# One load of two DRAM rows into both partition halves, made into two loads of one row each

## The chip, the cores and the metric

The kernel runs on one core of one Trainium2 chip. The metric is the device time of the whole program in microseconds (us). Engines are named as the profile names them: PE (TensorE, matrix products), DVE (VectorE), ACT (ScalarE), POOL (GpSimd), and SP (SyncE), which here does nothing but issue DMAs. "DMA engines" are the sixteen units that move the bytes.

## The reference, cut to what matters

An encoder of two layers on 1024 positions of width 1024. Layer 0 is a gated long convolution (Hyena), layer 1 a bidirectional Mamba-2 scan (SSD) with 32 heads in 4 groups, done in 8 chunks of 128 positions in both directions. Each layer has an input projection, the mixer, an output projection and a layer norm. The change lies in layer 1, in the part of the scan that reads the carried state:

```
a_cs = jnp.cumsum(adt, axis=-1)
...
y_off = jnp.einsum('bctgn,bcghpn,bcght->bctghp', cc, prev_states, jnp.exp(a_cs))
return (y_diag + y_off).reshape(b, L, h, p)
```

For one group, one chunk and one direction, `exp(a_cs)` is an array of 8 heads by 128 positions. It multiplies the product of state and `cc`, which has 8 heads by 64 channels by 128 positions.

## The kernel before, in words

All products are fp32 (split into a high and a low part where accuracy asks for three passes). The program is one long stream: layer 0 (about the first 1075 us of the profile), its output layer, and then layer 1, in which the projections of layer 1 (`flow`, matmuls at L763), the scan (`ssd_back`, `ssd_forth`) and the first part of the output projection (`Out.steps`, matmuls at L1203) are interleaved so that PE always has projection matmuls between the small steps of the scan. `advance` sets how many projection steps stand between two steps of the scan. The framework's scheduler then fixes one order for each engine; each engine, SP too, works its list strictly in order. All DMAs of the scan are issued by SP, in one list, but for small ones of POOL.

In the scan heads lie in pairs: partition 64*o + p of a tile holds channel p of head 2*i + o, with i (0 to 3) and the 128 positions along the row. So the exponentials of the even heads (o = 0) must stand on each of the partitions 0 to 63, and those of the odd heads (o = 1) on each of 64 to 127.

- `ssd_dt` computes the exponentials once and writes them by `spread` (L970) to the DRAM array `ecd`, of shape [direction, group, chunk, o, i, position]. One (direction, group, chunk) is two rows, o = 0 and 1, of 512 numbers, 2 KB each.
- `ssd_decay` (L1027 to L1032) loads such a pair of rows into a tile `ec` of 128 x 512 (256 KB), each row copied to 64 partitions. It is called once for each chunk but one, in 4 groups and 2 directions: 56 loads. Two buffers are there for each direction.
- `ssd_offset` (L1034 to L1041) multiplies: four matmuls at L1038, then one DVE multiplication at L1040 that reads `ec`. It is the only reader.

Names in the other lines that the prediction touches: `bxd` is a DRAM array into which the projected x, B and C are written (L980, L993), from which `bx` is loaded (L1002) and used by DVE at L1008 (`xw`); `ybd` holds the backward direction's result (stored L1105, loaded L1124); `y` is stored at L1162 and read back by the output projection as `tr` (L1317); `wr` is a raw weight block of 512 KB (L219), split by ACT (L227, L233) and DVE (L228, L234). L679 and L681 are the convolution on DVE and the SiLU on ACT whose result PE transposes at L988. L1073 and L1099 are matmuls of the scan's inner part, L1143 to L1160 the norm of its result.

Of the kernel before, what the change touches and what calls it, by code (L numbers as in the profile page):

```python
# [192 lines left out]
class Build:  # L193
# [833 lines left out]
    def ssd_decay(self, p, t, g, c, d):  # L1027

        ec = self.values(self.pb if d else p, f"ec{d}", 2).rearrange("p (i n) -> p i n", i=4)
        src = t["ecd"][d, g, c].rearrange("o i n -> o (i n)").unsqueeze(1).broadcast_to([2, 64, 512])  # L1030
        self.nc.sync.dma_start(out=ec.rearrange("p i n -> p (i n)"), in_=src)
        return ec  # L1032

    def ssd_offset(self, pool, g, c, state, bc, ec):  # L1034
# [515 lines left out]
```

## Time and profile before

| | us |
|---|---|
| median of 3 runs | 2164.39 |
| lowest and highest | 2164.05, 2165.11 |
| the profiled execution's own time | 2173.37 |
| its span, first to last instruction | 2171.6 |
| PE busy in the span | 2089.6 (96%) |
| DVE, ACT, POOL busy | 1567.9, 1136.4, 324.8 |

The profiled execution is 0.4% longer than the median of the runs. PE is busy nearly always, so what sets the time shows in its 82 us of idle time and in the stretches in which it works at the lower of its two clocks. Durations in the prediction are those of the profiled execution.

### The profile page before, as it was taken

To read this page: it belongs to the slowest core of one execution; us is meant where nothing else is said; L and a number is where in the kernel's file an instruction comes from. 1 tells how busy PE (TensorE), PEld (TensorE's weight loads), DVE (VectorE), ACT (ScalarE), POOL (GpSimd) and SP (SyncE) were. 2 spreads that over 40 slices of the span, in tenths; PEclk is the share of its full clock that TensorE was granted. 3 is DMA by queue.
4 is the path that set the end of the run, shared out by engine and by line. 5 is a ranking of instruction groups with operands and counts; after the bars stand their busy time and mean duration, and the time that the engine had idled before them with its cause. 6 is when DMAs were issued, how large, how long until landed. Compare 5 with 4: busy or idle time off the path is not lost.

```text
span 2171.6 us, 28748 instructions
## 1 busy us (share of the span) xinstructions
PE 2089.6 (96%) x9930; PEld 1661.5 (77%) x9930; DVE 1567.9 (72%) x2268; ACT 1136.4 (52%) x1665; POOL 324.8 (15%) x385
## 2 busy tenths in 40 slices
PE   7999999999999999999999998999999999989897
PEld 5777777888888888888777776776777777767676
DVE  7999977676777777767766564664777777667575
ACT  4787866465656556556544343554455555432231
POOL 0000000000000000000000101244344344433120
PEclk9999999999999999999999999999999999989998
DMA  6277887665656556556776325343454555557652
GB/s 208 103 237 249 266 263 240 202 197 168 199 165 186 171 159 194 182 181 197 270 275 217 121 66 157 110 122 119 124 154 150 168 160 162 161 172 245 229 174 93
DMA packets 269631, 391.92 MB, mean 180 GB/s; under 512 B 31767, under 2 KB 168727, under 8 KB 268845
## 3 DMA queue, kind: packets, MB, share of 16 engines
q1 hardware_dynamic: 255741, 382.99, 55.8%
q0 software_dynamic: 13744, 7.09, 1.4%
q8 instruction: 79, 1.29, 0.2%
q14 instruction: 67, 0.55, 0.1%
HBM read 269.10 MB, written 120.85 MB: 180 GB/s over the span
## 4 chain that ended last, share of the span: by engine, by line
PE 74%; DMA 11%; DVE 8%; ACT 3%; issue 2%; SPq 1%; POOL 1%; POOLq 0%; DVEq 0%; ACTq 0%
PE pj L270 28%; PE pj L763 16%; PE pj L1203 8%; PE f L250 3%; PE f L252 3%; PE f L251 3%; DMA wr<-l_w_out 2%; PE f L1038 2%; PE pk L1203 2%; DMA tr<-y 2%; PE f L1015 1%; PE f L1099 1%; PE f L1073 1%; DMA bxd<-tr 1%; DVE wl L234 1%
## 5 line engine op out<-in xcount | busy, mean ns | idle before, releaser
L270 PE MATMUL pj<-xth,wh 128*128 128x512 f32 x1024 | 326.5, 398 | 1.8 <-ACT xth L233 1.8
L270 PE MATMUL pj<-xtl,wh 128*128 128x512 f32 x1024 | 326.5, 396 | 1.4 <-DVE xtl L234 1.4
L270 PE MATMUL pj<-xth,wl 128*128 128x512 f32 x1024 | 324.8, 394 | 0.0
L234 DVE TENSOR_TENSOR wl<-wr,wh 128x1024 fp32r<-128x1024 f32 x152 | 192.2, 1267 | 139.6 <-ACT wh L233 138.8
L233 ACT CAST wh<-wr 128x1024 fp32r<-128x1024 f32 x152 | 159.4, 1049 | 165.7 <-PE pj L1203 58.5
L270 PEld LDWEIGHTS pj<-xtl,wh 128*128 128x128 f32 x1024 | 192.7, 189 | 45.7 <-DVE xtl L234 2.4
L270 PEld LDWEIGHTS pj<-xth,wl 128*128 128x128 f32 x1024 | 193.0, 189 | 44.2 <-issue 0.5
L270 PEld LDWEIGHTS pj<-xth,wh 128*128 128x128 f32 x1024 | 189.4, 189 | 42.2 <-ACT xth L233 3.4
L763 PE MATMUL pj<-h1th,wh 128*128 128x512 f32 x640 | 212.8, 406 | 0.9 <-DVE cv L679 0.9
L763 PE MATMUL pj<-h1tl,wh 128*128 128x512 f32 x640 | 203.8, 395 | 0.0
L763 PE MATMUL pj<-h1th,wl 128*128 128x512 f32 x640 | 202.8, 394 | 0.0
L234 DVE TENSOR_TENSOR xl<-bs,xh 128x512 fp32r<-128x512 f32 x192 | 129.7, 687 | 51.9 <-ACT xh L233 51.1
L233 ACT CAST xh<-bs 128x512 fp32r<-128x512 f32 x192 | 117.8, 621 | 69.8 <-DMA bs<-vs 28.7
L763 PEld LDWEIGHTS pj<-h1th,wh 128*128 128x128 f32 x640 | 117.6, 189 | 38.6 <-issue 15.8
L567 DVE SCALAR_TENSOR_TENSOR cv<-pj,cw,cv 128x960 f32<-128x960 f32 x192 | 139.3, 745 | 4.9 <-ACT cv L564 2.8
L763 PEld LDWEIGHTS pj<-h1tl,wh 128*128 128x128 f32 x640 | 120.8, 189 | 26.9 <-issue 1.5
L763 PEld LDWEIGHTS pj<-h1th,wl 128*128 128x128 f32 x640 | 121.1, 190 | 25.7 <-issue 0.2
L1187 POOL TENSOR_SCALAR rs<-mv 128x1 f32<-128x1 f32 x16 | 6.3, 395 | 896.5 <-DMA yr<-y 707.9
L679 DVE SCALAR_TENSOR_TENSOR cv<-pj,cw,cv 128x1023 f32<-128x1023 f32 (+1 forms) x96 | 122.6, 1277 | 5.8 <-ACT cv L676 5.2
L1086 POOL TENSOR_TENSOR m<-m,dm 128x512 f32<-128x512 f32 x64 | 93.9, 1466 | 74.2 <-DVE m L1078 73.7
L1081 POOL TENSOR_TENSOR dm<-ident,dco 128x512 f32<-128x512 f32 x64 | 69.5, 1086 | 189.3 <-DVE dco L1066 137.2
L389 DVE TENSOR_TENSOR kr<-f,dec 64x512 f32<-64x512 f32 x128 | 87.9, 687 | 3.6 <-ACT dec L386 1.1
(292 smaller groups left out, 4195.4 us busy)
## 6 DMA issues: line engine op xcount, KB each, us to landing
wr<-w SPq DMA_DIRECT2D x104, 512.0 KB
k<-kd SPq DMA_DIRECT2D x256, 128.0 KB
wr<-l_w_out SPq DMA_DIRECT2D x64, 512.0 KB
ask<-asb SPq DMA_DIRECT2D x64, 256.0 KB
bs<-ask SPq DMA_DIRECT2D x64, 256.0 KB
kd<-asb SPq DMA_DIRECT2D x64, 256.0 KB
as<-asb SPq DMA_DIRECT2D x64, 256.0 KB
bs<-as SPq DMA_DIRECT2D x64, 256.0 KB
```

What stands on the lines that cost most here:

```text
L233: self.nc.scalar.copy(h, src)
L234: self.nc.vector.tensor_tensor(out=l, in0=src, in1=h.bitcast(F32), op=ALU.subtract)
L250: mm(out, ah, bh, start=start, stop=False)
L251: mm(out, ah, bl, start=False, stop=False)
L270: self.nc.tensor.matmul(ps[:, t], lhs[:, k], rhs[:, k, t], start=st, stop=sp)
L389: (nc.gpsimd if 2 * q + i in PM else nc.vector).tensor_tensor(out=ks[q ^ i][r], in0=ps[r], in1=dec[r], op=ALU.mult)
L567: nc.vector.scalar_tensor_tensor(out=acc[:, o], in0=ps[:, i], scalar=cw[:, w:w + 1], in1=acc[:, o], op0=ALU.mult, op1=ALU.add)
L679: nc.vector.scalar_tensor_tensor(out=acc[:, o], in0=ps[:, i], scalar=cw[:, w:w + 1], in1=acc[:, o], op0=ALU.mult, op1=ALU.add)
L763: nc.tensor.matmul(ps[:, c], lhs[:, k], rhs[k // 4][:, k % 4, c], start=st, stop=sp)
L1081: nc.gpsimd.tensor_tensor(out=dm, in0=self.ident.unsqueeze(1).broadcast_to([128, 4, 128]), in1=dco[:, h4:h4 + 4].unsqueeze(2).broadcast_to ...
L1086: nc.gpsimd.tensor_tensor(out=m, in0=m, in1=dm, op=ALU.add)
L1203: self.nc.tensor.matmul(po[hf], lhs[:, t], rhs[:, 512 * hf:512 * hf + 512], start=s, stop=e)
```

## The change: two loads in place of one

```
     def ssd_decay(self, p, t, g, c, d):
 
         ec = self.values(self.pb if d else p, f"ec{d}", 2).rearrange("p (i n) -> p i n", i=4)
-        src = t["ecd"][d, g, c].rearrange("o i n -> o (i n)").unsqueeze(1).broadcast_to([2, 64, 512])
-        self.nc.sync.dma_start(out=ec.rearrange("p i n -> p (i n)"), in_=src)
+        for o in range(2):
+            src = t["ecd"][d, g, c, o].rearrange("i n -> (i n)").unsqueeze(0).broadcast_to([64, 512])
+            self.nc.sync.dma_start(out=ec[64 * o:64 * o + 64].rearrange("p i n -> p (i n)"), in_=src)
         return ec
```

The source of the old load has three dimensions, 2 rows x 64 repeats x 512 numbers; that of each new load has two, 64 repeats x 512 numbers. The same bytes go to the same places. Lines below L1031 move down by one. The numbers of instructions on PE, DVE, ACT and POOL stay; SP issues 56 DMAs more.

SP's list at the start of the scan, before (names: `ec_...` is one buffer of the tile, `dwh` the exponentials in SBUF, the rest as above; a trailing x2 means two alike in a row):

```order
L970 DMA ecd<-dwh 8x4x128 x4
L1031 DMA ec_13935<-ecd 128x1x512
L1031 DMA ec_14115<-ecd 128x1x512
L219 DMA wr<-w 128x1024
L993 DMA bxd<-tr 128x4x128 x2
L1002 DMA bx<-bxd 128x896
```

SP's list at the same place with the change:

```order
L970 DMA ecd<-dwh 8x4x128 x7
L219 DMA wr<-w 128x1024
L1032 DMA ec_13942<-ecd 64x512 x2
L1032 DMA ec_14124<-ecd 64x512 x2
L993 DMA bxd<-tr 128x4x128 x2
L1002 DMA bx<-bxd 128x896
```

Each load has become two of 64 rows, and the weight load `wr` has moved ahead of them; the two stores of `tr` still stand behind them.

SP's list some 560 us later, in the output projection's stretch, before (`wr<-l_w_out` is a weight block of the output projection):

```order
L219 DMA wr<-l_w_out 128x1024
L1031 DMA ec_17283<-ecd 128x1x512
L1162 DMA y_68<-y 128x4x128
L1031 DMA ec_17289<-ecd 128x1x512
L219 DMA wr<-l_w_out 128x1024
L1124 DMA y<-ybd 128x512
```

And with the change:

```order
L219 DMA wr<-l_w_out 128x1024
L1032 DMA ec_17324<-ecd 64x512 x2
L1163 DMA y_68<-y 128x4x128
L1032 DMA ec_17331<-ecd 64x512 x2
L219 DMA wr<-l_w_out 128x1024
L1125 DMA y<-ybd 128x512
```

Here nothing has moved but that each load is two. In the last 200 us of the scan a few neighbours on DVE, ACT and SP change places, and one matmul on PE (L1015) moves ahead of seven of L1203.

## Rows read from the trace of the kernel before

**Rows 1.** The page: busy time, and the chain that ended last by engine.

```profile
PE 2089.6 (96%) x9930; PEld 1661.5 (77%) x9930; DVE 1567.9 (72%) x2268; ACT 1136.4 (52%) x1665; POOL 324.8 (15%) x385
...
PE 74%; DMA 11%; DVE 8%; ACT 3%; issue 2%; SPq 1%; POOL 1%; POOLq 0%; DVEq 0%; ACTq 0%
```

**Rows 2.** Waits of PE, 1316 to 2103 us: total us, times, longest.

```profile
PE f L988 <- ACT cv L681: 15.4, 3, 9.7
PE f L1073 <- DVE ss L1153: 9.4, 3, 4.3
PE f L1151 <- POOL dwh L1147: 7.1, 1, 7.1
PE f L1073 <- DVE y L1160: 6.1, 5, 2.4
```

**Rows 3.** Chain in order of time, its DMA legs: start, us from issue to landing.

```profile
1319.29 7.89 DMA bxd<-tr
...
1340.13 10.81 DMA bxd<-tr
1350.96 2.99 DMA bx<-bxd
...
1494.90 8.35 DMA ybd<-y
1503.26 2.64 DMA y<-ybd
...
1894.83 9.90 DMA wr<-l_w_out
...
2074.88 11.71 DMA tr<-y
```

**Rows 4.** SP's timeline at three of these legs: start, us, line, operation.

```profile
1335.35 1.10 SPq L1031 DMA_DIRECT2D ec<-ecd  x2
1336.51 2.97 SPq L219 DMA_DIRECT2D wr<-w  x1
1339.58 3.30 SPq L993 DMA_DIRECT2D bxd<-tr  x2
...
1492.87 0.51 SPq L1031 DMA_DIRECT2D ec<-ecd  x1
...
1893.46 0.51 SPq L1031 DMA_DIRECT2D ec<-ecd  x1
1894.83 0.35 SPq L219 DMA_DIRECT2D wr<-l_w_out  x1
```

**Rows 5.** Windows in which mainly such DMAs ran; the last two numbers: DMA share, GB/s.

```profile
64.25:65.25 1.00, 1.00 (x6) 0.76 (x5) 1.00 (x3) 1.00 (x3) 0.00 (x0) 1.00 0.57 178
211.50:212.30 0.80, 0.80 (x6) 0.63 (x5) 0.80 (x3) 0.80 (x1) 0.00 (x0) 1.00 0.87 330
...
1462.00:1464.00 2.00, 2.00 (x22) 1.48 (x20) 0.00 (x0) 0.00 (x0) 0.00 (x0) 1.00 0.13 47
```

**Rows 6.** Issues on SP by line: ns least/median/most.

```profile
L1031 SPq DMA_DIRECT2D ec<-ecd x56: 486/507/859, 1316.4 to 2074.3; - x56
...
L367 SPq DMA_DIRECT2D bs<-l_filt_w_out x16: 472/568/596, 15.5 to 214.7; - x16
```

**Rows 7.** Windows by stage: us, then busy PE, PEld, DVE, ACT, POOL; clock, DMA, GB/s.

```profile
1316.00:1530.00 214.00, 198.63 (x973) 153.31 (x971) 117.91 (x157) 101.27 (x128) 72.25 (x76) 0.95 0.40 120
1530.00:1820.00 290.00, 286.36 (x1496) 221.29 (x1495) 223.39 (x315) 148.58 (x194) 123.19 (x131) 0.99 0.51 154
1820.00:2103.00 283.00, 256.36 (x1272) 199.86 (x1272) 187.71 (x301) 100.84 (x148) 93.35 (x104) 0.96 0.62 194
1970.00:2045.00 75.00, 74.36 (x387) 59.19 (x387) 44.66 (x74) 17.84 (x31) 19.16 (x23) 1.00 0.71 228
```

**Rows 8.** The six windows at half clock from 1316 to 2103, three and their sum.

```profile
1351.40:1361.60 10.20, 3.03 (x11) 2.76 (x12) 3.85 (x4) 2.23 (x3) 0.00 (x0) 0.50 0.75 246
1515.40:1525.50 10.10, 9.17 (x24) 6.53 (x25) 3.59 (x7) 6.09 (x9) 1.81 (x2) 0.50 0.38 105
1566.50:1569.90 3.40, 3.40 (x10) 2.62 (x9) 3.40 (x6) 0.49 (x1) 0.00 (x0) 0.50 0.28 99
...
sum 44.00, PE 31.15 PEld 24.12 DVE 26.86 ACT 17.86 POOL 8.83; mean PE 5.19 PEld 4.02 DVE 4.48 ACT 2.98 POOL 1.47
```

**Rows 9.** The chain in the first output layer, which has no such loads.

```profile
1063.92 2.61 DMA yr<-y
...
1078.41 8.74 DMA wr<-l_w_out
1090.43 8.18 DMA yr<-y
```

**Rows 10.** SP's own waits, 1316 to 2103 us: total us, times, longest.

```profile
SPq L1031 <- DVE y L1040: 38.9, 24, 8.6
...
SPq L970 <- DMA ec<-ecd: 3.3, 1, 3.3
```

## The prediction

> **What bounds the kernel now.** I began with the page [rows 1]: PE is busy 96% of the span and holds 74% of the chain that ended last, but 11% of that chain is DMA. In a kernel bound by PE those DMA legs are the places where PE ran out of work. So next I asked who kept PE waiting in the stretch in which the changed loads are issued, 1316 to 2103 us. The windows by stage [rows 7] give its idle time: 214.0 - 198.6 = 15.4 us up to 1530, 290.0 - 286.4 = 3.6 us up to 1820, 283.0 - 256.4 = 26.6 us up to 2103, together 45.6 us. The table of PE's waits [rows 2] names ACT, DVE and POOL as releasers. None of them is the cause: the chain in order of time [rows 3] shows that behind them stand DMAs that took 8 to 12 us from issue to landing. The same kinds of DMA need 2.6 to 3.0 us elsewhere in that chain (the two `bx` and `y` legs in the same group).
>
> SP's timeline [rows 4] shows what these long legs share: each was issued just behind an `ec` load. The stores of `tr` at 1339.58 stand behind two of them, the store of `ybd` at 1494.90 two microseconds behind one, the weights at 1894.83 one microsecond behind one. And the windows [rows 5] show what an `ec` load does. At 1462 to 1464 one ran alone: the DMA share is 0.13 of sixteen engines, that is two engines, and they moved 47 GB/s. Its 256 KB (262144 bytes) at 47 GB/s take 5.6 us. So the two-row load runs on two engines, one for each row, it seems, and whatever is split over all engines behind it waits for these two. A DMA of 2.6 to 3.0 us becomes one of 8 to 9 us (8.35 in [rows 3]), and two `ec` loads in a row make it 11 (10.81).
>
> **The change, part by part.** *The shape.* Each load becomes two of 64 rows. The trace has a repeated source, the 128-row load of `delta`, which filled 64.25 to 65.25, and loads of 64 rows into tile halves from SP, which filled 211.5 to 212.3 [rows 5]. They ran at shares of 0.57 and 0.87, so on at least 9 and 14 engines, at 178 and 330 GB/s. At these rates the 256 KB of an `ec` pair take 1.5 or 0.8 us in place of 5.6. I take the worse, which shares the repeated source: every `ec` load keeps the engines 4 us less, and all sixteen alike, so that a DMA behind it is late by 1 to 1.5 us and not by 5 to 6.
>
> The Trainium skill speaks against this change. Its page "SBUF — State Buffer", section "Can I just issue two DMAs to hit both halves?", says that a DMA on half the partitions reaches half the ports and that two such DMAs serialize (it measured 6% more than one), and the rules of "DMA: Bandwidth & Descriptors" advise one transfer of 128 partitions. By that rule the gain would be nothing and the sum the time before. It compares with a full-width load, though, and the row at 1462 shows that the old load isn't one. The same page on DMA, section "Why a DMA increments its semaphore by 16 and not by 1", says that a DMA gets the largest number of engines up to 16 that divides the slowest dimension of both sides: 2 before, 16 after. The two engines at 1462 agree; that the new form gets 16, no run here shows yet.
>
> *The start of the scan, 1316 to 1530.* There 15.4 us of idle are the three waits for L681 [rows 2]: 11 us in two of them (behind the stores at 1319 and 1340), 4.4 in the third (behind `ybd` at 1494.90). After each PE fell to its lower clock of 1.2 GHz, shown as 0.50 [rows 8], in which it was busy 3.03 and 9.17 us; at 2.4 GHz that work takes half, so the clock costs another 6.1 us. With `tr` stored in about 3 us and not 8 and 11, the whole string from `tr` over `bx` to L1008 and L681 is done 7.89 + 10.81 - 2 x 3 = 12.7 us earlier, against 11 of idle; with `ybd` stored in 3 and not 8.35, DVE goes on 5 us earlier, against 4.4. Both stalls go, and nothing on PE is late next, since it has projection matmuls there. Term: 15.4 + 6.1 = **21.5 us**.
>
> *The middle, 1530 to 1820.* `ec` loads run here as everywhere, but PE is idle for 3.6 us alone; the waits are those for L1160 [rows 2], a burst of DVE work with no long DMA ahead of it. Also its window at half clock (3.40 us busy, 1.7 lost) stays. Term: **0**, at the most 3.6 + 1.7 = 5.3.
>
> *The end, 1820 to 2103.* Idle 26.6 us, and the other three windows at half clock hold 31.15 - 3.03 - 9.17 - 3.40 = 15.6 us of PE, which cost 7.8 [rows 8]. Of these 34.4 us some 2.5 are waits for L1160 that I leave, so 32 hang on long legs (`wr` of 9.90, `tr` of 11.71 [rows 3]). But here not all comes back. DVE is busy 188 of 283 us and the DMA share is 0.62 [rows 7]; with 25 us less for the same work both rise by a tenth, and the weight blocks of 512 KB delay each other without any `ec` load: in the first output layer legs of 8.74 and 8.18 us stand in the chain [rows 9]. On the other side, PE is busy 74.4 of 75 us in 1970 to 2045 at a DMA share of 0.71, the highest of the stages, so the share alone is no bound. Lower bound 0, upper bound 32; I take 70%, nearer the upper: **22 us**.
>
> *The added issues.* 56 more issues on SP, at the median of the 64-row loads 0.568 us [rows 6], make 32 us of SP's time in 787. SP waits far longer than that for others; its waits for L1040, which frees `ec`, alone come to 38.9 us [rows 10], and the second half doesn't wait again. A DMA behind a pair is issued 0.57 us later, which 4 us of earlier room cover; where the cover is thin I count **1 us** lost in all. Bounds: 0 and 32, if every issue lay on the path. The few neighbours that change places on DVE, ACT and SP I cost at nothing, for PE's list is the same but for one matmul; as bound either way I take the 6.1 us that the waits for L1160 [rows 2], which come from the order on DVE, cost in all.
>
> Sum: 21.5 + 22 - 1 = 42.5, rounded to 43. Against the profiled span, 2171.6 becomes 2129; the median of the runs is 9 us below the profiled execution, and the same 43 from 2164.4 give **2121 us**.
>
> **The rivals.** (a) *The end stays late.* The legs shrink, but the 512 KB weights, the `tr` loads and DVE keep PE waiting after 1820 as in [rows 9]. Then only the first term comes, with a little of the last: 21.5 to 26, or 2139 to 2143. For it: the busy DMA engines; against it: the stage at 0.71 with PE full.
>
> (b) *Everything comes back.* All 45.6 us of idle and 15.6 of clock, less a few: 55 to 60, so 2104 to 2109. For it: nearly every long leg in the chain is behind an `ec` load. Against it: DVE's own bursts.
>
> (c) *The halves serialize, or run on few engines too.* Then nothing lands sooner and the time is 2164, within 0.2%. Against it: 330 GB/s in [rows 5] for loads of the very shape. (This is what the page "SBUF — State Buffer" of the Trainium skill, as told above, would lead one to expect.)
>
> (d) *SP becomes the late one: slower.* SP works in order; 0.57 us more ahead of every DMA behind an `ec` load, and each extra DMA takes one of SP's completion semaphores, whose next user waits for its landing, as L970 did for an `ec` load, 3.3 us [rows 10]. A dozen legs of the chain, each later by 0.57, make 7 us, 2171; all 56 make 2196. It decides if the halves don't free the engines by at least 0.57 us sooner than the 5.6 of now, so only with (c).
>
> **How the numbers follow.** The forecast (gain 34 to 52, 2112 to 2130) gets 0.55, (a) 0.19, (b) 0.17, (c) 0.05, (d) 0.04. A measurement of this kernel can tell 0.2%, 4 us. Faster: 0.91; same: 0.05; slower: 0.04. The range reaches from (b)'s lower end, 2103, to (a)'s upper, 2143, and leaves out (c), (d) and the thin ends.
>
> **What would show it.** In the profile after: DMA share far over 0.13 while an `ec` pair runs alone; the legs `tr` at 1319 and 1340 and `ybd` at 1494 at 2.5 to 4 us; no idle of PE ahead of L988 before 1530, nor half clock; L970 not waiting for `ec`; PE idle from 1316 on down from 45.6 to about 15; L1160's waits still there. I am wrong if `ec` still occupies two engines, if `wr` and `tr` legs of 8 us and more remain in the last 200 us, or if PE's idle moves to waits for DVE.

## The result and the profile after

The changed kernel takes 2126.05 us (median of 4 runs, 2124.32 to 2128.08) against 2164.58 (2164.05 to 2165.11, 4 runs) before: a ratio of 0.9822, 95% interval 0.9805 to 0.9839, so 38.5 us faster. Timed again later beside other runs (the last experiment below) it took 2123.86 against 2169.34, ratio 0.9795 (0.9776 to 0.9814), 45.5 us faster. The profiled execution of the changed kernel took 2124.32 with a span of 2122.5.

The page of the changed kernel: busy time, and the chain that ended last by engine.

```profile
PE 2076.1 (98%) x9930; PEld 1654.5 (78%) x9930; DVE 1569.2 (74%) x2268; ACT 1136.8 (54%) x1665; POOL 326.6 (15%) x385
...
PE 84%; DVE 7%; DMA 3%; ACT 2%; issue 2%; POOL 1%; SPq 0%; POOLq 0%; DVEq 0%; ACTq 0%
```

Against [rows 1] PE's idle time in the span fell from 82 to 46 us, its busy time by 13.5 (the same 9930 matmuls, fewer of them at half clock), and the share of DMA in the chain from 11% to 3%. The other engines do the same work. Next the windows by stage. A stage is cut at the same matmuls of PE's list as in [rows 7], so that it holds the same work (the first count in brackets is PE's: 973, 1494 and 1273 here, 973, 1496 and 1272 there). The bounds 1316, 1530, 1820 and 2103 then lie at 1312.9, 1505.4, 1795 and 2054.

```profile
1312.90:1505.40 192.50, 192.50 (x973) 149.35 (x971) 117.57 (x157) 101.31 (x128) 71.90 (x76) 1.00 0.45 133
1505.40:1795.00 289.60, 286.49 (x1494) 221.29 (x1495) 222.25 (x315) 148.57 (x194) 124.98 (x132) 0.99 0.52 155
1795.00:2054.00 259.00, 250.73 (x1273) 196.97 (x1271) 190.54 (x301) 102.21 (x148) 94.47 (x104) 0.99 0.68 210
```

The first stage is 21.5 us shorter, the second 0.4, the third 24.0. Another 3.1 us were won before the first of the changed loads went out, and none after 2103: together 49.0 of the 49.1 us by which the span is shorter. Idle time of PE is length less busy time: 0 in the first stage (15.4 before), 3.1 in the second (3.6), 8.3 in the third (26.6). The rest is clock: in these stages the changed kernel has three half-clock windows and not six [rows 8], none of them in the first.

```profile
1542.10:1545.50 3.40, 3.40 (x10) 2.62 (x9) 3.40 (x7) 0.71 (x1) 0.00 (x0) 0.50 0.43 154
1876.60:1880.00 3.40, 3.04 (x11) 2.85 (x12) 3.40 (x7) 3.37 (x6) 1.02 (x2) 0.50 0.97 331
1927.80:1931.20 3.40, 3.40 (x10) 2.62 (x9) 1.89 (x3) 0.63 (x1) 2.03 (x3) 0.50 0.82 253
sum 10.20, PE 9.84 PEld 8.09 DVE 8.69 ACT 4.71 POOL 3.04; mean PE 3.28 PEld 2.70 DVE 2.90 ACT 1.57 POOL 1.01
```

The load itself: the first line is a stretch in which, but for a few small packets, the four halves of two `ec` tiles ran alone; then SP's timeline around two of the legs of [rows 3 and 4] (start, us, line, operation).

```profile
1330.30:1332.30 2.00, 2.00 (x12) 1.52 (x11) 0.39 (x1) 1.06 (x1) 0.00 (x0) 1.00 0.98 251
```

```profile
1327.76 2.42 SPq L1032 DMA_DIRECT2D ec<-ecd  x4
...
1333.20 0.92 SPq L993 DMA_DIRECT2D bxd<-tr  x2
...
1336.47 0.33 SPq L1002 DMA_DIRECT2D bx<-bxd  x1
...
1479.13 0.33 SPq L1106 DMA_DIRECT2D ybd<-y  x1
...
1482.35 1.27 SPq L1125 DMA_DIRECT2D y<-ybd  x3
```

The halves fill 0.98 of the sixteen engines where the old load filled 0.13 [rows 5], at 251 GB/s in place of 47. At this rate the 256 KB of a pair take 1.0 us in place of 5.6, between the 0.8 and 1.5 of the prediction. The two stores of `tr` still stand behind four halves, and the load of `bx` that needs them goes out 3.3 us after the first of them (11.4 before, 1339.58 to 1350.96 in [rows 4 and 3]); the load of `y` goes out 3.2 us after the store of `ybd` (8.35 before).

What is left shows in PE's waits (1312.9 to 2054: total us, times, longest) and in the chain's DMA legs after 1780 (start, us).

```profile
PE f L1074 <- DVE y L1161: 4.5, 4, 2.4
PE f L1152 <- POOL dwl L1148: 1.8, 2, 0.9
PE f L1160 <- ACT rs L1157: 1.7, 1, 1.7
PE f L1152 <- POOL dwh L1148: 1.2, 1, 1.2
```

```profile
1807.67 4.93 DMA bx<-bxd
...
1916.68 5.85 DMA bx<-bxd
...
1985.25 5.70 DMA y<-y
1992.01 2.81 DMA ec<-ecd
2001.13 5.79 DMA wr<-l_w_out
```

The 15.4 us for L988 of [rows 2] are gone, the waits for the norm's DVE work (L1160, now L1161) are not (6.1 us before, 4.5 now), and no DMA leg of this part of the chain is longer than 6 us.

### The profile page after: what moved, and what is told of

It reads as the page before. It is cut to its first block, busy times and chain, and to the rows that moved or that the text cites. A ratio compares the mean times of both kernels' runs of the same rounds, so it can differ in the third digit from the quotient of the medians.

```text
span 2122.5 us, 28822 instructions
## 1 busy us (share of the span) xinstructions
PE 2076.1 (98%) x9930; PEld 1654.5 (78%) x9930; DVE 1569.2 (74%) x2268; ACT 1136.8 (54%) x1665; POOL 326.6 (15%) x385
## 4 chain that ended last, share of the span: by engine, by line
PE 84%; DVE 7%; DMA 3%; ACT 2%; issue 2%; POOL 1%; SPq 0%; POOLq 0%; DVEq 0%; ACTq 0%
PE pj L270 32%; PE pj L763 19%; PE pj L1204 9%; PE f L250 3%; PE f L252 3%; PE f L251 3%; PE f L1039 2%; PE pk L1204 2%; PE f L1015 2%; PE f L1100 1%; PE f L1074 1%; DMA wr<-l_w_out 1%; DVE wl L234 1%; PE f L988 1%; PE f L383 1%
## 5 line engine op out<-in xcount | busy, mean ns | idle before, releaser
L270 PEld LDWEIGHTS pj<-xtl,wh 128*128 128x128 f32 x1024 | 192.7, 189 | 45.6 <-DVE xtl L234 2.1
L763 PE MATMUL pj<-h1th,wh 128*128 128x512 f32 x640 | 212.1, 405 | 0.9 <-DVE cv L679 0.9
L763 PE MATMUL pj<-h1tl,wh 128*128 128x512 f32 x640 | 202.6, 393 | 0.0
L763 PE MATMUL pj<-h1th,wl 128*128 128x512 f32 x640 | 202.0, 393 | 0.0
L763 PEld LDWEIGHTS pj<-h1th,wh 128*128 128x128 f32 x640 | 117.2, 188 | 38.2 <-issue 15.6
L763 PEld LDWEIGHTS pj<-h1tl,wh 128*128 128x128 f32 x640 | 120.0, 188 | 26.8 <-issue 1.5
L763 PEld LDWEIGHTS pj<-h1th,wl 128*128 128x128 f32 x640 | 120.1, 188 | 25.4 <-issue 0.2
```

The source lines that it names most:

```text
L270: self.nc.tensor.matmul(ps[:, t], lhs[:, k], rhs[:, k, t], start=st, stop=sp)
L763: nc.tensor.matmul(ps[:, c], lhs[:, k], rhs[k // 4][:, k % 4, c], start=st, stop=sp)
```

## The experiments

Theory A, the prediction's: what counts is on how many DMA engines a load of `ec` runs, because what stands behind a load on few engines waits for these. What the kernels vary for it is the slowest (outermost) dimension of the load's source, which is 2 before and 64 in each half of the change. Theory B: the cut itself helps, since two smaller DMAs, and the new order that the scheduler made of SP's, DVE's and ACT's lists, let other work in between. Six kernels keep the computation and write each exponential eight times to DRAM, with the same bytes loaded; then the number of engines and of loads can be chosen apart. Of each kernel the lines are shown that take the place of the old load; `m = 16 * d + 4 * g` is the first of the four rows of a direction and group. The store is the same in the six (one DMA of 32 x 8 x 128 in the place of 8 x 4 x 128):

```
-                nc.sync.dma_start(out=t["ecd"][:, :, c, o].rearrange("d g i n -> (d g) i n"),
-                                  in_=ec[r + o:r + 64:2, 128 * (c % 4):128 * (c % 4) + 128])
+                nc.sync.dma_start(out=t["ecd"][c, o].rearrange("k m n -> m k n"),
+                                  in_=ec[r + o:r + 64:2, 128 * (c % 4):128 * (c % 4) + 128].unsqueeze(1).broadcast_to([32, 8, 128]))
```

**One load on two engines** (as before, from copy 0; the lists of PE, DVE and ACT as before but for a handful of rows, SP's too but that the first `ec` loads and the `ecd` stores stand elsewhere):

```
+        src = t["ecd"][c, :, 0, m:m + 4].rearrange("o i n -> o (i n)").unsqueeze(1).broadcast_to([2, 64, 512])
```

> Control. The exponentials are written to DRAM in eight copies (16 stores of 128 KB in place of 16 KB), and one load of two rows x 64 repeats reads the first copy, as before. Theory A (the old load runs on two DMA engines, and all that is issued behind it waits for these two): the load is as narrow as before, so the time stays at 2164, plus 0 to 8 us for the larger stores at the start of the scan. Theory B (two issues instead of one, with the order that the scheduler then chooses, are what helps): also 2164 plus the stores. DMA share 0.13 while a load runs alone.

**Two loads on two engines** (64 rows each, from two copies; the lists of DVE and ACT as in the change but for a handful of rows):

```
+        for o in range(2):
+            src = t["ecd"][c, o, :2, m:m + 4].rearrange("k i n -> k (i n)").unsqueeze(1).broadcast_to([2, 32, 512])
+            self.nc.sync.dma_start(out=ec[64 * o:64 * o + 64].rearrange("p i n -> p (i n)"), in_=src)
```

> Two loads of 64 rows, as in the change, with the engine orders of the change, but each load's source is two copies x 32 repeats, so its slowest dimension is 2. Theory A: each half still runs on two engines; no gain, 2164 to 2175, slower than the control by up to 7 us for the added issues, DMA share 0.13 while a pair runs alone. Theory B: the whole gain, 2124 to 2135.

**One load on all engines** (sixteen rows, each repeated eight times; the lists of SP, DVE, ACT and POOL are those of the one load on two engines, row for row):

```
+        src = t["ecd"][c, :, :, m:m + 4].rearrange("o k i n -> (o k) (i n)").unsqueeze(1).broadcast_to([16, 8, 512])
```

> One load of 128 rows, in the engine orders of before, whose source is sixteen rows (two exponentials x eight copies) x 8 repeats. Theory A: it spreads over sixteen engines; the gain of the change without the split, 2120 to 2135 (up to 4 us better than the change for 56 issues fewer, up to 8 worse for the larger stores). Theory B: one issue and the old order, so 2164 and more.

**Two loads on all engines** (the change's own loads, from copy 0; those lists are again the ones of the two loads on two engines):

```
+        for o in range(2):
+            src = t["ecd"][c, o, 0, m:m + 4].rearrange("i n -> (i n)").unsqueeze(0).broadcast_to([64, 512])
+            self.nc.sync.dma_start(out=ec[64 * o:64 * o + 64].rearrange("p i n -> p (i n)"), in_=src)
```

> The fourth corner: two loads of 64 rows on sixteen engines, with the stores in eight copies. Theory A (engines used): within 8 us of the one wide load, 2120 to 2132, and over 30 below the two narrow loads. If the split by itself also cost the 9 us by which two narrow loads were slower than one narrow one, it is 2132; if that difference came from narrow loads queueing twice, it is 2123 to 2126.

| us, median (range; ratio to before with interval) | few engines | all engines |
|---|---|---|
| one load | 2154.72 (2153.76 to 2159.94; 0.9937, 0.9916 to 0.9958) | 2123.29 (2120.49 to 2124.61; 0.9791, 0.9773 to 0.9810) |
| two loads | 2164.11 (2158.92 to 2169.33; 0.9978, 0.9964 to 0.9991) | 2122.99 (2121.25 to 2124.21; 0.9782, 0.9761 to 0.9802) |

The two loads on all engines were timed beside runs of the kernel before at 2170.4 us, the other three beside runs at 2169.3.

Going from two engines to all gives 31.4 us with one load and 41.1 with two, with the same lists on each side. Cutting the load gives nothing with all engines (0.3 us) and loses 9.4 with few. So A is shown, and neither B's cut nor the change's lists of DVE and ACT are a gain of their own. Nor is it how many rows of DRAM a load reads: of the two loads the wide ones read one row each, the narrow ones two. Where the width counts can be seen in the first and the last stage, cut at the same matmuls, of one load on two engines and of one on all:

```profile
1317.40:1516.20 198.80, 194.18 (x975) 150.46 (x973) 118.48 (x156) 101.58 (x128) 71.52 (x75) 0.99 0.49 139
...
1807.30:2089.60 282.30, 259.25 (x1273) 202.26 (x1271) 186.30 (x301) 100.66 (x148) 94.01 (x104) 0.95 0.63 194
```

```profile
1316.70:1509.30 192.60, 192.60 (x975) 149.41 (x973) 117.09 (x156) 101.81 (x128) 71.36 (x75) 1.00 0.50 143
...
1797.10:2054.20 257.10, 249.69 (x1272) 195.87 (x1271) 188.64 (x301) 101.77 (x148) 97.21 (x104) 0.99 0.69 212
```

The last stage is 25.2 us shorter by width alone, the first only 6.2, for with one narrow load it is short already. That is the surprise in the first column, where no gain was expected: this kernel is 14.6 us below the runs of before beside it, and its first stage is 198.8 us long where the kernel before has 214.0. What fits this is SP's list:

```profile
1316.41 0.91 SPq L993 DMA_DIRECT2D bxd<-tr  x2
...
1328.08 0.59 SPq L1032 DMA_DIRECT2D ec<-ecd  x1
...
1346.22 0.34 SPq L1002 DMA_DIRECT2D bx<-bxd  x1
...
1356.86 0.53 SPq L1032 DMA_DIRECT2D ec<-ecd  x1
```

The first `ec` load goes out after the stores of `tr` at 1316 and not ahead of them, and the third, at 1356.86, behind the load of `bx`, where it stood ahead of the stores that this needs [rows 4]. So narrow loads that stand out of the way seem to do less harm; the larger stores differ too, and no run parts the two. Two narrow loads are 9.4 us worse than one mostly in the last stage (289.9 us against 282.3); whether the number of loads or the lists, which differ at once, make that isn't settled.

That the two loads were narrow shows in a stretch where one pair ran alone (two engines' share again):

```profile
1447.50:1449.50 2.00, 2.00 (x20) 1.53 (x20) 0.00 (x0) 0.00 (x0) 0.00 (x0) 1.00 0.13 49
```

**One load on four and on eight engines**, with the lists of one load on two, to see how the time goes with the width:

```
+        src = t["ecd"][c, :, ::4, m:m + 4].rearrange("o k i n -> (o k) (i n)").unsqueeze(1).broadcast_to([4, 32, 512])
```

> One load whose source is four rows (two copies of each) x 32 repeats, stores and engine orders as with one narrow load. Theory A: four engines, DMA share 0.25 while it runs alone, 256 KB in 2.8 us in place of 5.6. If a stall is as long as the excess over its cover, the 31 us between one narrow and one wide load are gained for the greater part, 2128 to 2140. Theory B: no change from one narrow load, 2150 to 2160.

```
+        src = t["ecd"][c, :, ::2, m:m + 4].rearrange("o k i n -> (o k) (i n)").unsqueeze(1).broadcast_to([8, 16, 512])
```

> One load whose source is eight rows x 16 repeats: eight engines, DMA share 0.5 while it runs alone, 1.4 us of transfer. Theory A: nearly all of the gain, 2121 to 2128. Theory B: 2150 to 2160.

They took 2131.99 us (2131.58 to 2134.16; 0.9827, 0.9803 to 0.9851) and 2126.93 (2122.35 to 2129.33; 0.9798, 0.9774 to 0.9822). Windows in which one such load ran alone, four engines, then eight, then the sixteen rows:

```profile
1447.50:1449.50 2.00, 2.00 (x21) 1.42 (x19) 0.00 (x0) 0.00 (x0) 0.00 (x0) 1.00 0.26 101
```

```profile
1419.10:1420.00 0.90, 0.90 (x6) 0.74 (x5) 0.90 (x2) 0.90 (x1) 0.00 (x0) 1.00 0.51 191
```

```profile
1434.50:1435.30 0.80, 0.80 (x5) 0.68 (x4) 0.80 (x1) 0.00 (x0) 0.80 (x1) 1.00 0.69 228
```

At 47 [rows 5], 101, 191 and 228 GB/s the 256 KB take 5.6, 2.6, 1.4 and 1.1 us. The first step, 3.0 us less for each of 56 loads, is worth 22.7 us; the second, 1.2 us, 5.1; the third 3.6, which the ranges of these runs don't separate from nothing. The rule that the prediction quoted from the Trainium skill's page "DMA: Bandwidth & Descriptors" (section "Why a DMA increments its semaphore by 16 and not by 1") agrees: slowest dimensions of 2, 4 and 8 gave shares of 0.13, 0.26 and 0.51, about 2, 4 and 8 sixteenths. With sixteen the share of 0.69 shows at least eleven engines; that it was all sixteen, this window doesn't show.

**Four loads of 32 rows** (from the stores of before; 224 loads in place of 56; the lists of PE, DVE and ACT differ from those of before in some fifty to sixty places each), for the price of an issue:

```
+        for o in range(4):
+            src = t["ecd"][d, g, c, o // 2].rearrange("i n -> (i n)").unsqueeze(0).broadcast_to([32, 512])
+            self.nc.sync.dma_start(out=ec[32 * o:32 * o + 32].rearrange("p i n -> p (i n)"), in_=src)
```

> Each load becomes four loads of 32 rows, 168 issues more than before and 112 more than the change. Theory A with a small price of issues: 2126 to 2132, since the engines carry the same bytes over all sixteen and SP has room. If issues cost on the path what they take on SP (0.57 us each), 2126 + 64 = 2190; if a third of them do, 2147.

It took 2121.92 us (2118.63 to 2124.87; 0.9777, 0.9754 to 0.9800), less than expected. SP's issues of `ec`, in the changed kernel and in this one (ns least/median/most; first and last start, us):

```profile
L1032 SPq DMA_DIRECT2D ec<-ecd x112: 444/587/1342, 1313.2 to 2027.9; - x112
```

```profile
L1032 SPq DMA_DIRECT2D ec<-ecd x224: 302/419/1482, 1315.5 to 2023.0; - x112
```

At the medians SP spends 28 us on these issues before (56 x 0.507, [rows 6]), 66 with the change and 94 with four loads, and the time doesn't follow. It is no better than the change in a way that can be told either: the intervals of the two ratios overlap (0.9754 to 0.9800 and 0.9776 to 0.9814).

**The kernel before, once more**, for a second profiled execution:

> The kernel before, profiled once more. The first profiled execution was 9 us longer than the median of the timed ones. If that lies in the stalls behind the two-engine loads (theory A), a span nearer 2163 shows less than 45.6 us of idle time of PE from the first such load to the last, or fewer windows at half clock; if in layer 0, the stretch up to 1316 us is shorter by as much.

It took 2165.38 us, with a span of 2163.6. Its windows in the same stages, cut at the same matmuls, and the sum of its six windows at half clock:

```profile
1313.70:1525.10 211.40, 196.80 (x974) 152.07 (x972) 118.50 (x157) 101.28 (x128) 71.58 (x75) 0.97 0.40 121
1525.10:1813.40 288.30, 284.83 (x1495) 220.13 (x1495) 224.30 (x315) 148.47 (x194) 122.04 (x132) 1.00 0.52 155
1813.40:2095.00 281.60, 259.34 (x1272) 202.70 (x1271) 186.61 (x301) 100.75 (x148) 92.77 (x104) 0.95 0.62 194
```

```profile
sum 44.20, PE 32.62 PEld 24.83 DVE 27.57 ACT 17.95 POOL 10.97; mean PE 5.44 PEld 4.14 DVE 4.60 ACT 2.99 POOL 1.83
```

PE's idle is 14.6 + 3.5 + 22.3 = 40.3 us here, against 45.6 in the execution that the prediction used. The stalls at the end vary from one execution to the next.

**The cut in one part of the loads alone**, the other loads and all stores as before: the 7 loads of the backward direction's first group, the 28 loads that follow by group, and the 21 of the last groups. With the 28 all lists are those of before, but for the added issues and one `wr` that stands one load further forward; with the 7 SP's list at the start, and with the 21 the lists at the end, are those of the change. The conditions are:

```
+        if d == 1 and g == 0:
...
+        if not (d == 1 and g == 0) and g < 2 + d:
...
+        if g >= 2 + d:
```

> Only the seven loads of the backward direction's first group are split (about 1316 to 1500 us); the other 49 stay as before, and the orders of PE, DVE, ACT and POOL are those of before. The prediction's first term says 21.5 us: 2139 to 2147. The rival that the loads at the start are of no account says 2164.

> Only the 28 loads of the middle are split (the forward direction of groups 0 and 1, the backward one of groups 1 and 2). The prediction's term is 0, at the most 5.3: 2159 to 2168. If these loads count as the others do, half of the gain: 2145.

> Only the 21 loads of the end are split (the forward direction of groups 2 and 3, the backward one of group 3). The prediction's term is 22 us, bounds 0 and 32: 2142 (2132 to 2150). Rival (a), in which the weight blocks of 512 KB and DVE keep this stage late anyway, says 2160 to 2165.

| | us, median (range) | ratio (interval) | less than before (2168.43) |
|---|---|---|---|
| first 7 | 2158.57 (2155.26 to 2165.1) | 0.9959 (0.9939 to 0.9979) | 9.9 |
| next 28 | 2153.99 (2152.72 to 2157.04) | 0.9936 (0.9919 to 0.9953) | 14.4 |
| last 21 | 2145.35 (2141.07 to 2147.31) | 0.9897 (0.9880 to 0.9915) | 23.1 |

The three sum to 47.4, close to the 45.5 of all 56 in the later timing, so the parts don't depend much on each other. The expectations of the first two were missed: 2158.6 lies above the 2139 to 2147 that the prediction's term gave, and 2154.0 below 2159 to 2168. Windows of the first stage and of the last, cut at the same matmuls, for the three kernels in this order:

```profile
1314.00:1517.70 203.70, 195.56 (x975) 151.49 (x973) 118.16 (x157) 101.34 (x128) 72.14 (x76) 0.98 0.43 126
...
1805.10:2085.30 280.20, 256.33 (x1272) 199.64 (x1271) 186.80 (x301) 100.72 (x148) 93.40 (x104) 0.96 0.63 195
```

```profile
1314.30:1512.30 198.00, 194.36 (x974) 150.69 (x972) 118.08 (x157) 101.25 (x128) 71.89 (x76) 0.99 0.44 129
...
1803.10:2084.90 281.80, 257.32 (x1273) 201.19 (x1271) 187.32 (x301) 100.49 (x148) 94.19 (x104) 0.95 0.62 194
```

```profile
1315.30:1526.10 210.80, 197.85 (x973) 152.80 (x971) 120.68 (x157) 101.13 (x128) 71.33 (x76) 0.96 0.41 121
...
1816.00:2070.70 254.70, 248.49 (x1273) 195.51 (x1271) 188.40 (x301) 102.34 (x148) 96.29 (x104) 0.99 0.69 214
```

The last 21 loads repair the last stage, where idle falls to 6.2 us from 26.6, and hardly anything else. The 28 of the middle repair the first stage, where idle falls to 3.6 from 15.4, more than the first 7 do (8.1). Four of them are issued in it already: the pair of [rows 4] at 1335.35, in front of the leg of 10.81 us, and the load at 1492.87, in front of the leg of 8.35, are among them.

**The change once more**, beside runs of the kernel before on another chip:

> The changed kernel itself once more, timed in five rounds beside the kernel before. The variants with four loads of 32 rows, and with one or two wide loads and stores in eight copies, came to 0.978 to 0.979 of the kernel before; the change to 0.982 in its first timing. If issues and stores are free and the engines used are all that counts, the change comes to 0.978 to 0.980 here too, 2121 to 2126; if the variants are better by a mechanism of their own, it stays at 0.982 and above the 2123 of the variants.

The median was 2123.86 us (2121.58 to 2126.68, 5 runs); before took 2169.34 (2162.46 to 2172.03, 9 runs).

## Why the prediction was right, and where it was off

**The start, 21.5 us: right.** Idle went from 15.4 to 0 and the half clock from 6.1 us to none, which is the term exactly, and the stage is 21.5 us shorter. The runs add whose loads it was: those of the middle more than the start's own. How much of it the width did, and how much the new place of the `ec` loads in SP's list, shows roughly at one leg, from the issue of the first of two stores of `tr` to that of the load of `bx`. The kernel with 7 split loads has the change's list here and narrow loads ahead of the stores (first fence); the one with 28 has wide loads there and the list of before, but for the one `wr` (second).

```profile
1328.77 1.11 SPq L1036 DMA_DIRECT2D ec<-ecd  x2
1334.39 1.70 SPq L993 DMA_DIRECT2D bxd<-tr  x2
1343.75 0.33 SPq L1002 DMA_DIRECT2D bx<-bxd  x1
```

```profile
1335.58 1.08 SPq L1033 DMA_DIRECT2D ec<-ecd  x2
1336.76 1.08 SPq L993 DMA_DIRECT2D bxd<-tr  x2
1341.95 0.33 SPq L1002 DMA_DIRECT2D bx<-bxd  x1
```

The leg takes 9.4 us in the first and 5.2 in the second, against 11.4 before and 3.3 with the change. With either list the width takes some 6 us off, and the list some 2.

**The middle, 0: right.** Idle 3.6 became 3.1, and the window at half clock of 3.40 us stayed, with the waits for the norm's DVE work. This holds for the stage; the loads that the code counts to it gave 14.4 us, in the first stage.

**The end, 22 us: right, with some luck.** Idle fell from 26.6 to 8.3, 18.3 us, and the clock's cost from 7.8 to (3.04 + 3.40) / 2 = 3.2: together 22.9; the stage is 24.0 us shorter. That most of the 32 us hung on the `ec` loads is what the runs show. The 70% were a guess between 0 and 32, and executions differ by more than its distance: in the one profiled in the last experiment this stage takes 254.5 us, 28.5 less than before.

```profile
1796.70:2051.20 254.50, 248.60 (x1272) 195.46 (x1271) 190.44 (x301) 102.05 (x148) 95.53 (x104) 0.99 0.69 214
```

What stays are waits for the norm and legs of 5 to 6 us, of `bx`, `y` and `wr`. That these DMAs delay each other, at a share of 0.68 in this stage, is the prediction's reason for them; no run here tests it.

**The added issues, -1 us: too small to be told from nothing.** Two wide loads against one, 0.3 us; four against two, less than the runs tell apart. The bound of 32 us is ruled out.

**The rivals.** (a), an end that stays late, falls by the run that cut the last 21 loads alone (23.1 us). (b), that all comes back, falls short: 11.4 us of idle are left. (c), serialized halves, falls by the share of 0.98 and by the equal times of one and two wide loads; the advice against two DMAs for two halves in the Trainium skill's page "SBUF — State Buffer", section "Can I just issue two DMAs to hit both halves?", agrees with these equal times, in that the cut by itself gave nothing, and doesn't bear on a load that ran on two engines. (d), a late SP, falls with the 224 loads.

**What was off: the last step, "the same 43 from 2164.4".** The span of the profiled execution fell by 49.1 us, of which 3.1 were already there when the first changed load went out (the matmul at L763 that waits 0.86 us for `cv` starts at 1313.65 before and at 1310.52 after). Its idle and half clock in the three stages fell by 21.5 + 0.5 + 22.9 = 44.9, near the forecast's 43. The median fell by 38.5 in the same comparison, so 2126 came and not 2121. The execution profiled first was 9 us above the median, and part of that lay in the very stalls that the change removes. The second profiled execution, at the time of the medians, has 40.3 + 32.62 / 2 = 56.6 us of idle and half clock, 4.6 less than the 45.6 + 15.6 of the first, in a span that is 8.0 shorter. From 56.6 to the 11.4 + 9.84 / 2 = 16.3 of the changed kernel it is 40.3, and 2164.4 - 40.3 is 2124.1. A gain read from an execution that is slow in those stalls belongs to that execution's time. That this is the whole of the difference isn't shown: 5 us are within what the kernel before varies. Its medians in the later timings were 2168.4 to 2170.4, and from one of these the change took 45.5, more than the 43.

## What to carry to other kernels

When a small DMA takes three times as long as its kind, look at what stands ahead of it in the queue and at the DMA share while that one runs alone: two engines' share can mean, as it did here, that a broadcast has too short a slowest dimension, and the price is paid by what stands behind it. Cut or reshape so that the dimension is long; whether it took one piece, two or four made no difference here, where SP had slack. Place a gain by the stretch in which the transfers run, not by the loop that issues them, since a list may issue some of them early; to compare a stage of two kernels, cut it at the same instructions and not at the same times. And subtract a gain from the time of an execution in which the stall had that size.

## What the hardware showed that was not expected

The time falls steeply with the first doubling of a load's engines and hardly with the last: 2154.7, 2132.0, 2126.9 and 2123.3 us for two, four, eight and all, with the same lists. One load of sixteen rows showed a share of only 0.69 at 228 GB/s, the four halves of two tiles together 0.98 at 251, and the times of the kernels agree all the same. Executions of the kernel before lay between 2162 and 2176 us (42 of them), those of the changed one between 2121 and 2129; with nine of the latter it isn't shown that the time varies less without the stalls.
